# Decoder step on one core: a third staging tile for weights, and other places for weight splits and low parts around the layer norms

## The chip, the cores and the metric

The kernel runs on one core of one Trainium2 chip. The metric is device time in microseconds (us) of one execution; lower is better. The kernel before took 1143.75 us (median of three runs, 1142.8 to 1144.4).

A core has four engines that compute: TensorE (PE, matrix products), VectorE (DVE), ScalarE (ACT) and GpSimd (POOL). Each works through its own queue in order. SyncE (SP) issues the transfers between device memory and the on-chip memory. Semaphores connect the queues.

## The reference

One inference step of a decoder with two layers, in float32, on 512 prompt tokens and 8 single new tokens (520 columns), width 1024:

```
for i in range(2):
    m = attention(x) if i == 0 else gla(x)          # token mixer, with w_o
    x = layer_norm(ALPHA * x + m, ln_mix_g[i], ln_mix_b[i])
    h = x @ w_up;  a, u = halves of h               # 1024 -> 2 x 2816
    c = conv_b + causal depthwise conv, width 3, of a
    x = layer_norm(ALPHA * x + (gelu(c) * u) @ w_down, ln_ffn_g[i], ln_ffn_b[i])

layer_norm(x): mu = mean(x); var = mean((x - mu)^2)
               (x - mu) * rsqrt(var + 1e-5) * g + b
```

Layer 0 mixes tokens with sliding-window attention (16 heads, 2 key-value heads, window 128, rotary positions, sinks), layer 1 with gated linear attention (GLA, 4 heads). The caches, the GLA states and the last rows of the convolution are outputs too.

## The kernel before, in words

**Layout.** Activations lie transposed: 128 partitions hold a chunk of 128 features, 8 chunks (`KD`) make the width, and the tokens run along the free dimension. The tokens are cut in two groups, a (256 prompt tokens) and b (256 prompt tokens and the 8 samples).

**Split operands.** Matrix products run in a faster 32-bit format (`F32R`) that drops low bits. So each operand is kept as a high part (the value rounded to that format) and a low part (the value less its high part), and a product is three matmuls for each chunk: high by high, high by low, low by high (`product`, lines 193 to 196; `product2` joins the first two for group a, lines 214 and 215). For group a's first product of an FFN, `product` does all the high-by-low matmuls last (line 198).

**Units of weights.** The work is a list of units, each with one 128-column piece of a weight matrix (512 KB where it has 8 chunks). `load_unit` transfers it to a staging tile `raw` (line 160), ScalarE makes the high part `wh` (165) and VectorE the low part `wl` (168). There are `RAWS = 2` staging tiles and `WSLOTS = 6` pairs of `wh` and `wl`. A new load waits until the low part that last read its staging tile is done; a high part waits until PE has finished with its pair.

**Order.** `order` writes the sequence by hand: group a runs up to five units ahead of b within a phase, and at the end of a phase b's last units come in a row before a's first unit of the next phase. Each unit takes one slot. When b has done unit u, `next_unit` loads unit u + 6. Steps that come later are generators: each `yield n` puts the rest off by n slots (`spawn`, `due`); with `yield 0` it comes behind what is already waiting in the same slot.

This sequence is only a priority. A scheduler then lays out each engine's queue at compile time by a model of the timing: when an engine is free it takes the first step in the sequence that the model holds ready. `issue_after(ins)` ties what follows, on the engine of `ins` alone, behind `ins` in that engine's queue; it waits for nothing on other engines.

**Norms.** `ln_chunk` runs for each of the 8 chunks of the output projection (or the down projection): VectorE adds the product to x (243 or 245); after chunk 0 a first mean is taken off all chunks, held in the tiles `sb` and `sa` (251 to 258); from chunk 1 on the sum and the sum of squares over chunks grow, for group b on POOL except for the last chunk's (275, 276). Then `ln_end`: PE sums over partitions (283), ScalarE copies the mean (`mu`, 288), POOL and VectorE take it off (291, 299), VectorE and ScalarE work out the factor (292 to 305, with the exponential at 301). For each chunk VectorE then scales x (321), ScalarE adds the bias and rounds to the high part (322) and VectorE makes the low part (323).

**Weights around a norm.** A phase that begins at unit e follows a norm in three places: the FFN of layer 0, the GLA of layer 1, the FFN of layer 1. Units e + 1 to e + 5 are "late": their splits are put into the sequence one slot later, by `parts`, with the high part on ScalarE behind group a's exponential (line 177) and the low part on VectorE (179) behind a's last scaling (unit e + 1) or a's last low part (the others), as long as the slot is within `HOLD = 5` of a's norm. An FFN also holds one extra unit, e + 6, in a pair of its own; it is split without ties (165, 168).

Of the kernel before, what the change touches and what calls it, by code (L numbers as in the profile page):

```python
# [22 lines left out]
KD = 8  # L23
# [19 lines left out]
WSLOTS = 6  # L43
RAWS = 2
HIACT = 2
# [10 lines left out]
LATEB = 14  # L56

HOLD = 5

# [18 lines left out]
def parted(rows):  # L78

    return rows.rearrange("p (j t) -> p t j", t=2)  # L80
# [15 lines left out]
class Net:  # L96
# [53 lines left out]
    def load_unit(self, u, pieces=1, extra=False, late=False):  # L150
        src, nt = self.units[u][0], self.units[u][1]
        nc = self.nc
        if nt == 0:
            return self.load_rank(u)
        r = self.raw.tile([P, KD * P], F32, name="raw")
        pool = self.wx if extra else self.wts
        h, l = (pool.tile([P, KD * P], F32R, name=name) for name in ("wh", "wl"))
        n = nt * P // pieces
        for c in (slice(i * n, (i + 1) * n) for i in range(pieces)):
            nc.sync.dma_start(out=r[:, c], in_=src[:, c])  # L160
            if late:
                self.spawn(self.parts(u, h[:, c], l[:, c], r[:, c]), 1)
                continue
            if u >= HIACT:
                nc.scalar.activation(h[:, c], r[:, c], AF.Copy)  # L165
            else:
                nc.gpsimd.tensor_scalar(h[:, c], r[:, c], 1.0, 0.0, op0=ALU.mult, op1=ALU.add)
            nc.vector.tensor_tensor(l[:, c], r[:, c], h[:, c].bitcast(F32), op=ALU.subtract)  # L168
        self.w[u] = (h, l)

    def parts(self, u, h, l, r):


        norm = self.norm if self.norm and self.slot < self.norm[0] else None
        behind = lambda ins: self.tc.issue_after(ins) if norm else ExitStack()
        with behind(norm and norm[1]):
            self.nc.scalar.activation(h, r, AF.Copy)
        with behind(norm and norm[2 if u == norm[4] else 3]):
            self.nc.vector.tensor_tensor(l, r, h.bitcast(F32), op=ALU.subtract)  # L179
        yield from ()  # L180

# [47 lines left out]

    def next_phase(self):  # L230
        return min(p for p in self.phases if p > self.unit)


    def ln_chunk(self, g, m, ps, scaled, last=False):
# [7 lines left out]
        if scaled:  # L242
            nc.vector.tensor_tensor(x[:, m], x[:, m], ps, op=ALU.add)
        else:
            nc.vector.scalar_tensor_tensor(x[:, m], x[:, m], ALPHA, ps, op0=ALU.mult, op1=ALU.add)
        if m == 0:
            yield 1
            mp = self.mtile("sc")[:, :n]
            nc.tensor.matmul(mp, self.ones_a, x[:, 0], start=True, stop=True)
            sb = c("sb")  # L250
            nc.scalar.activation(sb, mp, AF.Copy, scale=float(KD))
            sa = sb
            if not scaled:
                sa = c("sa")
                nc.scalar.activation(sa, mp, AF.Copy, scale=KD / ALPHA)
# [19 lines left out]
        (nc.gpsimd if m < p1 else nc.vector).tensor_tensor(g.s1, x[:, 0] if m == 1 else g.s1, x[:, m], op=ALU.add)  # L275
        (nc.gpsimd if m < p2 else nc.vector).tensor_tensor(g.s2, g.s2, q, op=ALU.add)

    def ln_end(self, g, i, last=False):
# [25 lines left out]
        rp = r if last else e2  # L304
        nc.vector.scalar_tensor_tensor(rp, q, 1.5, r, op0=ALU.add, op1=ALU.mult)
        sc = lambda m: self.par[:, C_LNG + i * KD + m:C_LNG + i * KD + m + 1]
        bi = lambda m: self.par[:, C_LNB + i * KD + m:C_LNB + i * KD + m + 1]
        if last:
# [9 lines left out]
            return  # L318

        for m in range(KD):  # L320
            v = nc.vector.scalar_tensor_tensor(x[:, m], x[:, m], sc(m), rp, op0=ALU.mult, op1=ALU.mult)  # L321
            nc.scalar.activation(g.xh[:, m], parted(x[:, m]), AF.Identity, bias=bi(m))  # L322
            xl = nc.vector.scalar_tensor_tensor(g.xl[:, m], parted(x[:, m]), bi(m), g.xh[:, m].bitcast(F32), op0=ALU.add, op1=ALU.subtract)  # L323
        if g.i == 0:
            self.norm = self.slot + HOLD, self.exp, v.ins, xl.ins, self.next_phase() + 1
        for m in range(KD):
# [656 lines left out]

    def next_unit(self, extra):
        u = self.nu
        if u < len(self.units):
            self.nu += 1
            done = u - WSLOTS
            late = not extra and self.units[u][1] and any(e - 5 <= done < e for e in (*self.phases[2:3], *self.phases[3:4], *self.phases[5:6]))
            self.load_unit(u, extra=extra, late=late)  # L990
            if extra:
                self.extra[u] = True

    def run(self):
# [3 lines left out]
        self.attn_open()  # L998
        self.later, self.slot, self.seq, self.norm = [], 0, 0, None
        for i, u in self.order():  # L1000
            g = self.groups[i]
            _, _, f, a, pre = self.units[u]
            if i == 1:
                self.unit = u
            if i == 0 and pre:
                pre()
                if pre != self.gla_open:
                    for _ in range(EXTRA):
                        self.next_unit(True)
            self.slot += 1  # L1010
# [129 lines left out]
```

## Time and profile before

The profiled execution took 1145.38 us; its span, from the first to the last instruction, is 1143.7 us.

| | |
|---|---|
| median of three runs | 1143.75 us (1142.8 to 1144.4) |
| profiled execution | 1145.38 us, span 1143.7 us |
| PE busy | 1105.9 us, 97% of the span |
| VectorE busy | 784.1 us, 69% |
| ScalarE busy | 566.9 us, 50% |
| POOL busy | 321.8 us, 28% |
| moved by DMA | 122.81 MB, mean 107 GB/s |
| mean granted PE clock | 0.989 |

The page of the profile gives busy times, a chain of work and the costliest groups of instructions. A row of a group has line, engine, operation, output and inputs by name, shapes, count, busy time and mean. The view of waits has, for an engine: who waited for whom, the total in us, how many times, and the longest. A row of the timeline has start and duration in us, engine, line, operation, output and inputs, and in brackets the idle time of the engine just before and what ended it. A row of the windows view has a stretch, its length and, for PE, PEld (PE's weight loads), DVE, ACT and POOL, busy time and number of instructions; then the granted PE clock (1.00 is full speed), the share of the 16 DMA engines and GB/s. A matmul's end is modelled, and consecutive ones overlap, so starts are what to compare.

### The profile page before, as it was taken

The page shows a single profiled execution, that of the slowest core. Times are in us where ns is not written, and L with a number is a line of the kernel's source. Part 1 is how long each engine was busy: PE and PEld are TensorE (multiplying, and loading weights), DVE is VectorE, ACT ScalarE, POOL GpSimd, SP SyncE. Part 2 cuts the span into 40 slices and gives each one's busy share as a digit, 9 for nine tenths or more (in the row PEclk, how much of TensorE's full clock was granted, in tenths as well). Part 3 has the DMA queues.
Part 4 walks back from the last instruction along what each step waited for, and adds up shares of the span by engine and source line. Part 5 has one row for each costly group of instructions (what it writes and reads, how often), then busy time and mean ns, then how long its engine had stood idle before and what let it go on. Part 6 is the DMA issues. An engine that isn't in the chain of part 4 may idle for free.

```text
span 1143.7 us, 22908 instructions
## 1 busy us (share of the span) xinstructions
PE 1105.9 (97%) x8806; PEld 1056.7 (92%) x8806; DVE 784.1 (69%) x1628; ACT 566.9 (50%) x1251; POOL 321.8 (28%) x589
## 2 busy tenths in 40 slices
PE   8999998999999999999899999998999999999995
PEld 7997798999999999999899999898999999999994
DVE  8897578755665566568867877788755665566657
ACT  5677555534553245435545655455524553245433
POOL 4575584400110001255311100383400110011344
PEclk9999999999999999999899999999999999999998
DMA  7453022333323223242125355332333232232222
GB/s 239 150 178 93 16 75 93 111 93 119 103 93 109 94 95 109 75 132 96 56 87 162 114 176 173 118 101 92 111 98 125 93 109 95 93 112 93 75 64 75
DMA packets 53788, 122.81 MB, mean 107 GB/s; under 512 B 6792, under 2 KB 27312, under 8 KB 53680
## 3 DMA queue, kind: packets, MB, share of 16 engines
q1 hardware_dynamic: 51664, 119.61, 32.7%
q10 hardware_dynamic: 2016, 1.75, 0.5%
q8 instruction: 69, 1.13, 0.4%
q14 instruction: 39, 0.32, 0.1%
HBM read 108.67 MB, written 8.47 MB: 102 GB/s over the span
## 4 chain that ended last, share of the span: by engine, by line
PE 74%; DVE 12%; DMA 5%; ACT 3%; issue 2%; POOL 2%; SPq 0%; ACTq 0%; DVEq 0%; POOLq 0%
PE accp L214 15%; PE accp L195 15%; PE accp L193 15%; PE accp L196 15%; PE accp L215 8%; DMA vb<-dv 3%; DVE wl L168 1%; DVE xs_a L323 1%; DVE wl L179 1%; DMA raw<-in_w_up 1%; DVE sgla L877 1%; DMA raw<-in_w_qkv 1%; DVE x_a L321 1%; DMA qs<-hl 1%; PE pv L521 1%
## 5 line engine op out<-in xcount | busy, mean ns | idle before, releaser
L168 DVE TENSOR_TENSOR wl<-raw,wh 128x1024 fp32r<-128x1024 f32 (+2 forms) x174 | 210.5, 1212 | 110.5 <-ACT wh L165 109.9
L165 ACT ACTIVATE wh<-raw 128x1024 fp32r<-128x1024 f32 (+2 forms) x170 | 175.9, 1035 | 208.3 <-PE accp L195 187.2
L193 PE MATMUL accp<-xh_b,wh 128*128 128x264 f32 x976 | 271.7, 278 | 7.4 <-ACT xh_b L322 7.4
L195 PE MATMUL accp<-xl_b,wh 128*128 128x264 f32 x976 | 270.6, 278 | 0.0
L196 PE MATMUL accp<-xh_b,wl 128*128 128x264 f32 x976 | 270.5, 277 | 0.0
L214 PE MATMUL accp<-xs_a,wh 128*128 128x512 f32 x576 | 196.3, 382 | 0.0
L193 PEld LDWEIGHTS accp<-xh_b,wh 128*128 128x128 f32 x976 | 185.0, 190 | 8.3 <-ACT xh_b L322 7.8
L195 PEld LDWEIGHTS accp<-xl_b,wh 128*128 128x128 f32 x976 | 184.6, 189 | 2.5 <-issue 0.4
L196 PEld LDWEIGHTS accp<-xh_b,wl 128*128 128x128 f32 x976 | 184.4, 189 | 0.8 <-issue 0.6
L215 PE MATMUL accp<-xs_a,wl 128*128 128x256 f32 x576 | 145.4, 273 | 0.0
L193 PE MATMUL accp<-hh_b,wh 128*128 128x264 f32 x480 | 134.0, 279 | 1.7 <-ACT hh_b L221 1.2
L195 PE MATMUL accp<-hl_b,wh 128*128 128x264 f32 x480 | 134.4, 280 | 0.3 <-DVE hl_b L561 0.2
L196 PE MATMUL accp<-hh_b,wl 128*128 128x264 f32 x480 | 133.6, 278 | 0.0
L214 PEld LDWEIGHTS accp<-xs_a,wh 128*128 128x128 f32 x576 | 109.1, 189 | 11.4
L193 PE MATMUL accp<-xs_a,wh 128*128 128x256 f32 x400 | 113.6, 286 | 0.9 <-ACT wh L165 0.9
L196 PE MATMUL accp<-xs_a,wl 128*128 128x256 f32 x400 | 112.6, 284 | 1.4 <-DVE wl L168 0.8
L215 PEld LDWEIGHTS accp<-xs_a,wl 128*128 128x128 f32 x576 | 110.2, 191 | 1.9
L195 PE MATMUL accp<-xs_a,wh 128*128 128x256 f32 x384 | 109.0, 284 | 0.6 <-DVE xs_a L222 0.3
L193 PEld LDWEIGHTS accp<-hh_b,wh 128*128 128x128 f32 x480 | 91.5, 191 | 2.4 <-ACT hh_b L221 1.6
L195 PEld LDWEIGHTS accp<-hl_b,wh 128*128 128x128 f32 x480 | 91.3, 190 | 1.8 <-DVE hl_b L561 0.4
L196 PEld LDWEIGHTS accp<-hh_b,wl 128*128 128x128 f32 x480 | 91.4, 190 | 0.2
L225 POOL COPY hist<-aext 128x2 f32<-128x2 f32 x44 | 10.7, 244 | 276.8 <-DVE aext L608 274.0
(327 smaller groups left out, 2500.5 us busy)
## 6 DMA issues: line engine op xcount, KB each, us to landing
raw<-in_w_up SPq DMA_DIRECT2D x88, 512.0 KB, 3.4
raw<-in_w_down SPq DMA_DIRECT2D x32, 512.0 KB, 3.4
raw<-in_w_gla SPq DMA_DIRECT2D x24, 512.0 KB, 3.4
raw<-in_w_mix_o SPq DMA_DIRECT2D x16, 512.0 KB, 4.1
raw<-in_w_down SPq DMA_DIRECT2D x16, 384.0 KB, 3.0
qs<-hl SPq DMA_DIRECT2D x64, 64.0 KB, 2.1
sgla<-in_state_gla SPq DMA_DIRECT2D x16, 256.0 KB, 2.8
vb<-dv SPq DMA_DIRECT2D x16, 256.0 KB, 3.7
```

The source lines that it names most:

```text
L165: nc.scalar.activation(h[:, c], r[:, c], AF.Copy)
L168: nc.vector.tensor_tensor(l[:, c], r[:, c], h[:, c].bitcast(F32), op=ALU.subtract)
L179: self.nc.vector.tensor_tensor(l, r, h.bitcast(F32), op=ALU.subtract)
L193: nc.tensor.matmul(o, h[:, ks], xh, start=k == 0, stop=False)
L195: nc.tensor.matmul(o, h[:, ks], xl, start=False, stop=False)
L196: nc.tensor.matmul(o, l[:, ks], xh, start=False, stop=not tail and k == nt - 1)
L214: both = lambda: nc.tensor.matmul(o, h[:, ks], in_turn(rs[:, k].rearrange("p t q j -> p t (q j)")), start=k == 0, stop=last)
L215: low = lambda: nc.tensor.matmul(o[:, :P], l[:, ks], in_turn(rh[:, k]), start=False, stop=False)
L321: v = nc.vector.scalar_tensor_tensor(x[:, m], x[:, m], sc(m), rp, op0=ALU.mult, op1=ALU.mult)
L323: xl = nc.vector.scalar_tensor_tensor(g.xl[:, m], parted(x[:, m]), bi(m), g.xh[:, m].bitcast(F32), op0=ALU.add, op1=ALU.subtract)
L521: mm = nc.tensor.matmul(pv[64 * v:64 * v + 64, b * P:(b + 1) * P], self.vtok[:, kb, 64 * v:64 * v + 64], parts[v][w][:, b], start=i == 0, ...
L877: late(nc.vector.scalar_tensor_tensor(s[:, j], vb[:, j], kraw[:, b:b + 1], s[:, j], op0=ALU.mult, op1=ALU.add))
```

## The change

It does five things.

1. `RAWS` goes from 2 to 3: a third staging tile.
2. The tiles `sb` and `sa` of the first mean take the place of the later `nv` and `r` (same tags, one buffer each).
3. In `ln_end` the low parts of x come in a loop of their own, behind all scalings and high parts. For group a they are put off by three slots and tied, on VectorE, behind the latest add of group b, which at that point is that of b's seventh chunk.
4. Late units have a number j, 1 to 5, their distance from e, and the extra unit becomes late with j = 6. Their splits are put off by 1, 2, 2, 2, 1 and 0 slots and then come last in their slot.
5. Each j has its ties, on marks that both norms set. High parts on ScalarE: j = 1 behind a's exponential, 3 behind a's last high part, 5 and 6 behind b's exponential, 2 and 4 free. Low parts on VectorE: 1 behind a's last scaling, 2 behind a's last low part, 3 and 4 behind b's last sum of squares, 5 and 6 behind b's factor (line 305). `HOLD` and `next_phase` go.

```diff
-RAWS = 2
+RAWS = 3
...
             if late:
-                self.spawn(self.parts(u, h[:, c], l[:, c], r[:, c]), 1)
+                self.spawn(self.parts(late, h[:, c], l[:, c], r[:, c]), (0, 1, 2, 2, 2, 1, 0)[late])
                 continue
...
-    def parts(self, u, h, l, r):
-        norm = self.norm if self.norm and self.slot < self.norm[0] else None
-        behind = lambda ins: self.tc.issue_after(ins) if norm else ExitStack()
-        with behind(norm and norm[1]):
+    def parts(self, j, h, l, r):
+        for _ in range(3):
+            yield 0
+        behind = lambda what: self.tc.issue_after(self.marks[what]) if what in self.marks else ExitStack()
+        with behind({1: "exp_a", 3: "high_a", 5: "exp_b", 6: "exp_b"}.get(j)):
             self.nc.scalar.activation(h, r, AF.Copy)
-        with behind(norm and norm[2 if u == norm[4] else 3]):
+        with behind({1: "rows_a", 2: "low_a", 3: "sums_b", 4: "sums_b", 5: "factor_b", 6: "factor_b"}[j]):
             self.nc.vector.tensor_tensor(l, r, h.bitcast(F32), op=ALU.subtract)
-        yield from ()
...
-            sb = c("sb")
+            sb = c("nv")
...
-                sa = c("sa")
+                sa = c("r")
...
         for m in range(KD):
             v = nc.vector.scalar_tensor_tensor(x[:, m], x[:, m], sc(m), rp, op0=ALU.mult, op1=ALU.mult)
-            nc.scalar.activation(g.xh[:, m], parted(x[:, m]), AF.Identity, bias=bi(m))
-            xl = nc.vector.scalar_tensor_tensor(g.xl[:, m], parted(x[:, m]), bi(m), g.xh[:, m].bitcast(F32), op0=ALU.add, op1=ALU.subtract)
+            xh = nc.scalar.activation(g.xh[:, m], parted(x[:, m]), AF.Identity, bias=bi(m))
+        self.marks.update({"rows_" + g.name: v.ins, "high_" + g.name: xh.ins})
+
         if g.i == 0:
-            self.norm = self.slot + HOLD, self.exp, v.ins, xl.ins, self.next_phase() + 1
+            yield 3
+            yield 0
+        with ExitStack() if g.i else self.tc.issue_after(self.marks["add_b"]):
+            for m in range(KD):
+                xl = nc.vector.scalar_tensor_tensor(g.xl[:, m], parted(x[:, m]), bi(m), g.xh[:, m].bitcast(F32), op0=ALU.add, op1=ALU.subtract)
+        self.marks["low_" + g.name] = xl.ins
...
-    def next_unit(self, extra):
+    def next_unit(self, extra, late=0):
...
-            done = u - WSLOTS
-            late = not extra and self.units[u][1] and any(e - 5 <= done < e for e in (*self.phases[2:3], *self.phases[3:4], *self.phases[5:6]))
+            e = min((p for p in self.phases[2:4] + self.phases[5:] if p > u - WSLOTS), default=u)
+            late = late or (0 if extra else max(0, u - e))
...
                     for _ in range(EXTRA):
-                        self.next_unit(True)
+                        self.next_unit(True, WSLOTS)
```

More of the change, by code (lines that the diff above doesn't have):

```diff
@@ L56 @@
 LATEB = 14
-HOLD = 5
 WIDE = 4
@@ L228, in mtile @@
         return self.mps.tile([P, 512], F32, name=tag, bufs=2 if tag == "sc" else 1)
-    def next_phase(self):
-        return min(p for p in self.phases if p > self.unit)
     def ln_chunk(self, g, m, ps, scaled, last=False):
@@ L242, in ln_chunk @@
         if scaled:
-            nc.vector.tensor_tensor(x[:, m], x[:, m], ps, op=ALU.add)
+            add = nc.vector.tensor_tensor(x[:, m], x[:, m], ps, op=ALU.add)
         else:
-            nc.vector.scalar_tensor_tensor(x[:, m], x[:, m], ALPHA, ps, op0=ALU.mult, op1=ALU.add)
+            add = nc.vector.scalar_tensor_tensor(x[:, m], x[:, m], ALPHA, ps, op0=ALU.mult, op1=ALU.add)
+        self.marks["add_" + g.name] = add.ins
         if m == 0:
@@ L275, in ln_chunk @@
         (nc.gpsimd if m < p1 else nc.vector).tensor_tensor(g.s1, x[:, 0] if m == 1 else g.s1, x[:, m], op=ALU.add)
-        (nc.gpsimd if m < p2 else nc.vector).tensor_tensor(g.s2, g.s2, q, op=ALU.add)
+        self.marks["sums_" + g.name] = (nc.gpsimd if m < p2 else nc.vector).tensor_tensor(g.s2, g.s2, q, op=ALU.add).ins
     def ln_end(self, g, i, last=False):
@@ L304, in ln_end @@
         rp = r if last else e2
-        nc.vector.scalar_tensor_tensor(rp, q, 1.5, r, op0=ALU.add, op1=ALU.mult)
+        factor = nc.vector.scalar_tensor_tensor(rp, q, 1.5, r, op0=ALU.add, op1=ALU.mult)
+        self.marks.update({"exp_" + g.name: self.exp, "factor_" + g.name: factor.ins})
         sc = lambda m: self.par[:, C_LNG + i * KD + m:C_LNG + i * KD + m + 1]
@@ L998, in run @@
         self.attn_open()
-        self.later, self.slot, self.seq, self.norm = [], 0, 0, None
+        self.later, self.slot, self.seq, self.marks = [], 0, 0, {}
         for i, u in self.order():
@@ L1002, in run @@
             _, _, f, a, pre = self.units[u]
-            if i == 1:
-                self.unit = u
             if i == 0 and pre:
```

## The prediction

> **What bounds the kernel now.** I read the page first, then the waits of the matmul engine, then the stretches around the norms, then each engine's timeline inside them.
>
> ```profile
> span 1143.7 us, 22908 instructions
> PE 1105.9 (97%) x8806; PEld 1056.7 (92%) x8806; DVE 784.1 (69%) x1628; ACT 566.9 (50%) x1251; POOL 321.8 (28%) x589
> PE accp L193 <- ACT xh_b L322: 7.4, 2, 3.9
> PE accp L704 <- ACT v_a L771: 2.5, 1, 2.5
> PE accp L198 <- DVE xs_a L323: 0.5, 1, 0.5
> PE accp L193 <- ACT wh L165: 0.9, 2, 0.5
> PE accp L196 <- DVE wl L168: 0.8, 2, 0.5
> PE sc L473 <- ACT pr L490: 2.0, 4, 0.7
> ```
>
> TensorE (PE) is the bound: busy 97% of the span. Only its waits can be won back. The two largest groups (total, times, longest) are three waits in all, and each stands where one layer's second group of tokens (b) leaves a norm: attention to FFN, FFN to GLA, GLA to FFN. The windows view gives, for each, the idle stretch and the stretch behind it; the last row is a steady stretch for comparison (the number after POOL is the granted clock).
>
> ```profile
> 185.60:189.20 3.60, 0.14 (x2) 0.00 (x1) 3.60 (x7) 1.87 (x6) 1.98 (x4) 1.00 0.20 59
> 546.30:549.00 2.70, 0.18 (x3) 0.00 (x1) 2.65 (x10) 1.56 (x5) 0.66 (x1) 0.95 0.00 0
> 783.70:787.80 4.10, 0.16 (x3) 0.01 (x1) 4.10 (x8) 2.32 (x8) 2.48 (x5) 0.98 0.24 60
> 189.20:193.50 4.30, 4.30 (x25) 4.30 (x26) 4.30 (x12) 3.04 (x7) 0.00 (x0) 0.63 0.18 72
> 549.00:554.50 5.50, 5.50 (x18) 4.39 (x19) 5.50 (x16) 2.91 (x7) 0.00 (x0) 0.50 0.00 0
> 787.80:791.10 3.30, 3.30 (x14) 3.16 (x15) 3.30 (x10) 2.92 (x7) 0.00 (x0) 0.51 0.24 92
> 300.00:350.00 50.00, 50.00 (x380) 48.07 (x380) 32.43 (x63) 25.76 (x49) 5.55 (x22) 1.00 0.32 102
> ```
>
> Each gap is paid twice: as idle time, and again because PE comes back at a clock of 0.63, 0.50 and 0.51.
>
> Why is b's norm late? These are PE's sums over partitions for b (L283), then ScalarE's queue at all three norms:
>
> ```profile
> 175.32 0.71 PE L283 MATMUL tp<-s_b,ones_a 128*128 128x264 f32 x2 [0.42 <-DVE s_b L275]
> 536.58 0.61 PE L283 MATMUL tp<-s_b,ones_a 128*128 128x264 f32 x2
> 773.54 0.71 PE L283 MATMUL tp<-s_b,ones_a 128*128 128x264 f32 x2 [0.43 <-DVE s_b L275]
> 176.21 1.06 ACT L177 ACTIVATE wh<-raw 128x1024 fp32r<-128x1024 f32 x1 [1.96 <-DMA raw<-in_w_up]
> 178.88 1.06 ACT L177 ACTIVATE wh<-raw 128x1024 fp32r<-128x1024 f32 x1 [1.61 <-DMA raw<-in_w_up]
> 179.84 0.36 ACT L288 COPY mu<-tp 128x264 f32<-128x264 f32 x1
> 540.45 0.36 ACT L288 COPY mu<-tp 128x264 f32<-128x264 f32 x1
> 778.43 0.36 ACT L288 COPY mu<-tp 128x264 f32<-128x264 f32 x1
> ```
>
> At the first norm the mean was ready at 175.32 + 0.71 = 176.03, and its copy ran at 179.84. In between ScalarE stood in front of two weight high parts whose weights had not landed. The copy was queued behind them: 3.8 us lost. By the same subtraction it is 540.45 - 537.19 = 3.3 us at the second norm and 778.43 - 774.25 = 4.2 us at the third.
>
> **The change part by part.** *Weight parts behind marked steps.* Take the weights that follow the first of the next phase in order, 1 to 5, and the extra one, 6. High parts 5 and 6 now stand behind b's exponential on ScalarE, so they can't stand in front of the mean's copy. High part 4 has no such tie; only the third tile, below, gets it out of the way. On VectorE low parts 3 and 4 stand behind b's last sum, and 5 and 6 behind b's factor (L305). Before, VectorE ran this at the first norm:
>
> ```profile
> 165.82 1.21 DVE L179 TENSOR_TENSOR wl<-raw,wh 128x1024 fp32r<-128x1024 f32 x1
> 167.30 3.48 DVE L323 SCALAR_TENSOR_TENSOR xs_a<-x_a,par,xs_a 128x256 fp32r<-128x256 f32 x6
> 171.04 0.50 DVE L323 SCALAR_TENSOR_TENSOR xs_a<-x_a,par,xs_a 128x256 fp32r<-128x256 f32 x1
> 171.47 1.20 DVE L179 TENSOR_TENSOR wl<-raw,wh 128x1024 fp32r<-128x1024 f32 x1
> 172.94 1.43 DVE L179 TENSOR_TENSOR wl<-raw,wh 128x1024 fp32r<-128x1024 f32 x1
> 174.29 0.97 DVE L275 TENSOR_TENSOR s_b<-s_b,x_b 128x264 f32<-128x264 f32 x1
> 185.41 1.76 DVE L168 TENSOR_TENSOR wl<-raw,wh 128x1024 fp32r<-128x1024 f32 x1
> 187.43 0.43 DVE L305 SCALAR_TENSOR_TENSOR pv<-msq,r 128x264 f32<-128x264 f32 x1
> 188.10 2.08 DVE L321 SCALAR_TENSOR_TENSOR x_b<-x_b,par,pv 128x264 f32<-128x264 f32 x5
> ```
>
> Low part 3 (172.94) leaves the place in front of b's sums: 174.29 - 172.94 = 1.35 us. The extra weight's low part (185.41) leaves the place between b's statistics and its factor: 1.76 us. So b's x should be ready 3.8 + 1.35 + 1.76 = 6.9 us sooner at the first norm. PE needs it from where group a's six units end:
>
> ```profile
> 182.90 0.28 PE L193 MATMUL accp<-xs_a,wh 128*128 128x256 f32 x1
> 185.47 0.28 PE L196 MATMUL accp<-xs_a,wl 128*128 128x256 f32 x1
> 189.20 0.38 PE L193 MATMUL accp<-xh_b,wh 128*128 128x264 f32 x1 [3.46 <-ACT xh_b L322]
> ```
>
> That is 189.20 - 185.47 = 3.7 us sooner, so 3.2 us are to spare. At the second norm (no extra weight) 3.3 + 1.35 = 4.6 us stand against the 2.7 us of its window, 1.9 to spare. At the third 4.2 + 1.35 + 1.76 = 7.3 against 4.1. I take all three idle times as gone: 7.4 + 2.5 = 9.9 us. What comes next on PE is then b's own product at full rate.
>
> The clock that isn't lost: 4.30 x 0.37 = 1.6, 5.50 x 0.50 = 2.75 and 3.30 x 0.49 = 1.6 us. In the second stretch PE also waited on b's chunks one by one and on group a's GLA steps, so I take half there, 1.4. Rate term: 1.6 + 1.4 + 1.6 = 4.6 us, bounds 3.2 to 6.0.
>
> [...]
>
> *Group a's low parts behind b's seventh add.* One of the eight moves: it ran ahead of low part 1, now all come behind b's sixth and seventh adds. Beside other work six took 3.48 us, 0.58 each, so eight take 4.6. Starting some 0.8 us (two adds) after low part 1 ends at 167.0, they end near 172.4 rather than 171.54. PE reads them in the tail of a's first unit and in its second. Bounds: 0 (PE's order is laid anew) to 0.9 us a norm. Queued behind the seventh add are now these eight and low part 2; the add waits for b's seventh product, which PE finishes one unit before a's first begins, so the wait is over before VectorE gets there.
>
> *Low part 5 behind the factor.* Its weight is PE's from 182.90 on. The factor moves to 187.43 - 6.9 = 180.5 and ends by 181.0; a low part takes 1.2 us, so right behind it the part is done at 182.2 and costs nothing. Behind b's eight scalings (five take 2.08, eight 3.3) it is done at 185.5: 2.6 us of stall. Bounds 0 to 2.6 us a norm. VectorE has a gap of its own between factor and first scaling (187.86 to 188.10), which a ready part fills, so I expect the near end. For these two edits together I take 0.5 us a norm, the size of the wait that PE had on xs_a there (quoted above): 1.5 us.
>
> *Third staging tile.* A load now waits for the low part three weights back, not two. So high part 4's load waits for low part 1 (done at 167.0), not low part 2 (172.7).
>
> ```profile
> raw<-in_w_up SPq DMA_DIRECT2D x88, 512.0 KB, 3.4
> qs<-hl SPq DMA_DIRECT2D x64, 64.0 KB, 2.1
> SPq L160 <- DVE wl L168: 380.5, 81, 28.2
> 145.44 6.37 POOL L258 TENSOR_TENSOR x_b<-x_b,sa 128x264 f32<-128x264 f32 x7
> 157.97 0.42 DVE L292 SCALAR_TENSOR_TENSOR nv<-msq,pv 128x256 f32<-128x256 f32 x1 [1.22 <-ACT msq L289]
> ```
>
> With 3.4 us to landing it is there at about 170.5, ahead of the mean at 174.7 (176.03 - 1.35). That is what keeps high part 4 harmless. Elsewhere the bound is PE's pace, not the loads. PE's waits on wh and wl outside the norms are 0.9 + 0.8 = 1.7 us: gain 0 to 1.7, I take 0.5, as loads at the start can't all come sooner.
>
> *Scratch tiles sb and sa become nv and r.* Group a's nv (157.97) now has to wait until b's centring on POOL is over (151.81): 6.2 us of cover, cost 0. If POOL fell behind by more than that, a's norm would start late by the rest.
>
> *Sum.* The profiled execution took 1145.38 us (span 1143.7). 1145.4 - 9.9 - 4.6 + 1.5 - 0.5 = 1131.9. The median lies 1.63 us lower, 1143.75: forecast 1130.2 us.
>
> **The rivals.** *The stall moves to the weights' low parts.* Low part 5 misses the place right behind the factor at all three norms: 3 x 2.6 = 7.8 in place of 1.5, so 1130.2 + 6.3 = 1136.5 us. For it: VectorE is busy without a break from 185.6 to 193.5 (rows above). Against: the gap behind the factor.
>
> *The change doesn't do what it says.* The schedule puts high part 4, the untied one, ahead of the mean's copy with its load late; the wait shown at 178.88 stays, one weight earlier. Then about all the gain goes: 1143.7 us. Against: 170.5 lies 4 us ahead of 174.7.
>
> *Slower: loads in the way of the attention's transfers.* A 512 KB load issued one tile sooner lies in front of the four qs copies of a column on the same 16 DMA engines. There are 16 such steps (64 copies, four each). A load takes 3.4 us; if a third of it, 1.1 us, shows on PE each time, that costs 18 us: 1130.2 + 18 = 1148 us. It decides from 13.5 / 16 = 0.85 us a step. For: qs lands in 2.1 us, so a load ahead is felt. Against: PE waited for scores only 2.0 us in all 64 matmuls, and the queue already holds loads back 380.5 us for want of a free tile, at a pace that PE sets; a third tile shifts this once and adds no load.
>
> **How the numbers follow.** Forecast 0.70, stall at the low parts 0.15, no effect 0.08, slower 0.07. The forecast's own range: all bounds good, 1145.4 - 9.9 - 6.0 - 1.7 - 1.6 = 1126 us; all bad, with 2.6 and 0.9 us at one norm each, the smaller rate term and no gain at the start, 1145.4 - 9.9 - 3.2 + 3.5 - 1.6 = 1134. The first rival's range reaches on to 1139 (1136.5 with 0.9 us more at three norms), which makes 1126 to 1139; what is left out is the other two rivals and the tails. About 0.2% (2.3 us) can be told from no change here: faster 0.85, same 0.08, slower 0.07.
>
> **What would show it.** Right: no gap over 1 us on PE at the three places and a clock near 1.00 behind them; the mean's copy within 0.3 us of PE's sums for b; low parts 5 and 6 right behind L305. Wrong: PE waiting for wl of a's sixth unit (first rival), L177 still in front of the mean's copy, or longer waits at L473.

## The result and the profile after

The kernel after takes 1153.05 us (median of six runs, 1151.43 to 1154.91), the kernel before, beside it, 1144.08 us (1142.8 to 1147.53). The ratio is 1.0073, 95% interval 1.0058 to 1.0088: slower by 0.73%, where 1.2% faster was forecast. The profiled execution after took 1152.26 us. First its page (span and busy times), then the waits of the matmul engine (total, times, longest in us):

```profile
span 1150.6 us, 22919 instructions
PE 1110.7 (97%) x8806; PEld 1061.5 (92%) x8806; DVE 784.0 (68%) x1628; ACT 565.8 (49%) x1251; POOL 319.7 (28%) x589
```

```profile
PE accp L194 <- DVE wl L178: 3.6, 2, 1.8
PE accp L196 <- DVE xs_a L326: 2.5, 5, 0.9
PE accp L191 <- ACT hh_b L219: 2.2, 2, 1.7
PE accp L191 <- ACT wh L163: 1.9, 2, 1.4
PE accp L191 <- ACT xh_b L318: 1.3, 2, 1.0
PE accp L191 <- ACT wh L176: 1.2, 1, 1.2
```

The waits that the forecast wanted gone are gone: xh_b went from 7.4 to 1.3 us, and the 2.5 us on v_a are no longer among the large ones. In their place stand five others, grown or new, 6.7 us of them for parts of weights (wl 3.6, wh 1.9 and 1.2). The span grew by 6.9 us, and PE's busy time by 4.8 of them (1105.9 to 1110.7): most of the loss is matmuls at a lower clock (mean granted clock 0.989 before, 0.982 after), not idle time. The windows view shows where (after POOL comes the granted clock):

```profile
181.90:187.10 5.20, 1.24 (x7) 0.65 (x6) 5.17 (x11) 5.20 (x12) 0.42 (x2) 0.81 0.30 101
187.10:192.00 4.90, 4.90 (x23) 4.90 (x24) 4.90 (x13) 1.56 (x4) 0.00 (x0) 0.50 0.34 107
554.00:560.00 6.00, 5.45 (x26) 5.15 (x26) 1.52 (x3) 0.20 (x1) 0.00 (x0) 0.50 0.29 87
744.40:750.00 5.60, 5.35 (x28) 4.64 (x29) 4.60 (x9) 3.58 (x7) 0.98 (x1) 0.70 0.34 111
300.00:350.00 50.00, 50.00 (x378) 48.03 (x377) 32.96 (x63) 26.36 (x51) 6.22 (x23) 1.00 0.30 97
```

At the first norm PE now has three short gaps in 5.2 us, and then 4.9 us at half clock, more than the one gap of before (3.6 us, then 4.3 us at 0.63) had cost. The rest of the kernel (last row) runs as before.

Both traces have 8806 matmuls, so the start of the n-th of them can be compared through the whole span. The table gives by how much each stage (times of before) became longer or shorter, in us, for the kernel after and for experiments told below. It is one profiled execution each, and one execution can lie about 2 us from another in a stage: the kernel with the shared scratch alone, whose ratio can't be told from 1, shows -1.6 us to the first norm and -1.8 us at it. Verdicts go by the ratios.

| stage | after | swap | third tile alone | low 3, 4 free | low 5 free | late high parts |
|---|---|---|---|---|---|---|
| to the first norm, 0 to 170 | -0.1 | -0.3 | -0.2 | +0.2 | -0.8 | -1.7 |
| first norm, 170 to 200 | +1.0 | -2.3 | -2.6 | -4.3 | -2.2 | -4.3 |
| second norm and first GLA head, 530 to 575 | +2.2 | +0.9 | -2.3 | -2.4 | -1.2 | -3.1 |
| GLA, 575 to 738 | -1.7 | -1.2 | +2.3 | 0.0 | 0.0 | -0.1 |
| GLA's end, 738 to 746 | +4.3 | +4.6 | 0.0 | 0.0 | 0.0 | 0.0 |
| third norm, 746 to 800 | +0.9 | -1.2 | -1.6 | -2.3 | -1.7 | -3.9 |

Nothing moves between 200 and 530 or behind 800. So the loss of 6.6 us in the first column is that of norms that gained nothing and of one place that the prediction never looked at, the end of the GLA.

Why the norms gained nothing is seen on three engines. ScalarE's timeline after, at the first norm:

```profile
174.22 0.38 ACT L284 COPY mu<-tp 128x264 f32<-128x264 f32 x1
178.87 0.43 ACT L296 ACTIVATE r<-nv 128x264 f32<-128x264 f32 x1 [3.97 <-DVE nv L288]
179.77 1.28 ACT L623 ACT_TABLE_LOAD   x1
181.38 1.99 ACT L176 ACTIVATE wh<-raw 128x1024 fp32r<-128x1024 f32 x2
```

VectorE's, at the first norm, the second norm and the GLA's end:

```profile
173.46 0.43 DVE L272 TENSOR_TENSOR s_b<-s_b,sq 128x264 f32<-128x264 f32 x1
173.81 2.91 DVE L178 TENSOR_TENSOR wl<-raw,wh 128x1024 fp32r<-128x1024 f32 x2
176.64 0.97 DVE L613 SCALAR_TENSOR_TENSOR conv<-aext,par,conv 128x256 f32<-128x256 f32 x1
178.42 0.42 DVE L288 SCALAR_TENSOR_TENSOR nv<-msq,pv 128x264 f32<-128x264 f32 x1
182.31 0.44 DVE L301 SCALAR_TENSOR_TENSOR pv<-msq,r 128x264 f32<-128x264 f32 x1
182.66 1.22 DVE L178 TENSOR_TENSOR wl<-raw,wh 128x1024 fp32r<-128x1024 f32 x1
183.80 2.08 DVE L317 SCALAR_TENSOR_TENSOR x_b<-x_b,par,pv 128x264 f32<-128x264 f32 x5
185.79 1.22 DVE L178 TENSOR_TENSOR wl<-raw,wh 128x1024 fp32r<-128x1024 f32 x1
...
546.70 1.27 DVE L317 SCALAR_TENSOR_TENSOR x_b<-x_b,par,pv 128x264 f32<-128x264 f32 x3
547.90 1.69 DVE L326 SCALAR_TENSOR_TENSOR xl_b<-x_b,par,xh_b 128x264 fp32r<-128x264 f32 x4
549.52 0.68 DVE L725 TENSOR_TENSOR_SCAN dcum<-reset,dmn 128x256 f32<-128x256 f32 x1
...
742.04 0.88 DVE L880 SCALAR_TENSOR_TENSOR sgla<-vb,kraw,sgla 128x256 f32<-128x256 f32 x2 [1.98 <-DMA vb<-dv]
743.18 0.48 DVE L905 SCALAR_TENSOR_TENSOR sg<-tp,par,sg 128x256 f32<-128x256 f32 x1
```

And PE's, at the first norm and at the GLA's end:

```profile
183.43 0.38 PE L191 MATMUL accp<-xs_a,wh 128*128 128x256 f32 x1 [1.20 <-ACT wh L176]
184.90 0.39 PE L191 MATMUL accp<-xh_b,wh 128*128 128x264 f32 x1 [0.98 <-ACT xh_b L318]
187.07 0.58 PE L194 MATMUL accp<-xs_a,wl 128*128 128x256 f32 x1 [1.77 <-DVE wl L178]
...
744.31 0.49 PE L191 MATMUL accp<-hh_b,wh 128*128 128x264 f32 x2 [1.70 <-ACT hh_b L219]
```

The mean's copy stands at 174.22, 5.6 us sooner than the 179.84 of before. But nv, which needs it, comes at 178.42: VectorE first runs low parts 3 and 4 (2.9 us) and 1.8 us of the convolution's steps. So 4.2 us lie between mean and nv where before there were 1.3 (179.84 to 181.11, where nv starts in the trace of before). The second thing is in the two late parts. At 181.38 ScalarE makes two high parts in a row and VectorE two low parts, at 182.66 and 185.79. In the sequence the extra weight (6) stands ahead of weight 5: its generator was started in an earlier slot, so its parts come out one round sooner. PE needs weight 5 first, for a's sixth unit, and weight 6 only behind b's first. It waits for the second high part until 183.43 and for the second low part until 187.07. Of the 3.95 us that PE waits in this stretch 2.97 are for weight 5 and 0.98 for b's x, which comes 4.3 us sooner than before (184.90 for 189.20).

### The profile page after: what moved, and what is told of

Its sections match the earlier page's. It is cut to its first block, busy times and chain, and to the rows that moved or that the text cites. A ratio compares the mean times of both kernels' runs of the same rounds, so it can differ in the third digit from the quotient of the medians.

```text
span 1150.6 us, 22919 instructions
## 1 busy us (share of the span) xinstructions
PE 1110.7 (97%) x8806; PEld 1061.5 (92%) x8806; DVE 784.0 (68%) x1628; ACT 565.8 (49%) x1251; POOL 319.7 (28%) x589
## 4 chain that ended last, share of the span: by engine, by line
PE 74%; DVE 13%; ACT 3%; DMA 3%; issue 3%; POOL 2%; SPq 1%; ACTq 0%; DVEq 0%; POOLq 0%
PE accp L193 15%; PE accp L194 15%; PE accp L212 15%; PE accp L191 15%; PE accp L213 8%; DMA vb<-dv 2%; DVE wl L178 1%; DVE xs_a L326 1%; DVE wl L166 1%; DMA qs<-hl 1%; DVE x_b L317 1%; PE pv L524 1%; DVE sgla L880 1%; DVE x_a L317 1%; ACT pr L493 1%
## 5 line engine op out<-in xcount | busy, mean ns | idle before, releaser
L166 DVE TENSOR_TENSOR wl<-raw,wh 128x1024 fp32r<-128x1024 f32 (+2 forms) x172 | 206.3, 1201 | 104.4 <-ACT wh L163 103.5
L163 ACT ACTIVATE wh<-raw 128x1024 fp32r<-128x1024 f32 (+2 forms) x168 | 173.6, 1034 | 196.1 <-PE accp L193 194.6
L191 PE MATMUL accp<-xs_a,wh 128*128 128x256 f32 x400 | 115.8, 292 | 4.0 <-ACT wh L163 1.9
L193 PE MATMUL accp<-xs_a,wh 128*128 128x256 f32 x384 | 112.1, 293 | 0.3 <-DVE xs_a L220 0.2
```

What stands on the lines that cost most here:

```text
L191: nc.tensor.matmul(o, h[:, ks], xh, start=k == 0, stop=False)
L193: nc.tensor.matmul(o, h[:, ks], xl, start=False, stop=False)
```

## The experiments

Each is timed beside the kernel before, and the ratio is to that. None leaves out work. Letters in the texts on record name theories and rivals; theory A stands in each text for what that text says of it.

**Round one: which part of the change loses.** The swap gives the extra weight's generator one round more:

```diff
-        for _ in range(3):
+        for _ in range(3 + (j == WSLOTS)):
```

> One number is changed in the kernel after: the parts of the extra weight (6) are issued one round later in the program, so that they come behind those of weight 5, which the matmul engine needs first. Theory A (wrong order of two weights): in the kernel after, weight 6 went through ScalarE and VectorE ahead of weight 5 at the first and the third norm, and the matmul engine waited there for weight 5 (1.2 and 1.8 us at the first norm, 1.8 us at the third) and came back at half clock. Then this kernel takes 5 to 8 us less than the kernel after: 1145 to 1148 us, and the matmul engine's waits on the late wl (L178) go from 3.6 us to under 1 us. Rival B (VectorE's whole load in the window is the bound, whatever the order): 1151 to 1154 us, since the wait only passes from the weight to b's x.

Measured: 1146.22 us, ratio 1.0002 (0.9990 to 1.0015). The waits on L178 fell from 3.6 us to 1.0. That is 7 to 8 us from one number (6.8 by the medians, 0.71% by the ratios), so theory A holds. In the table 3.3 us of it stand at the first norm and 2.1 at the third; the 1.3 us at the second, which has no extra weight, are within what one execution varies. Much of it is clock: 0.982 to 0.985 in all executions of the kernel after, 0.988 to 0.995 with the swap. But it only brings the kernel back to before.

The third tile alone is the kernel before with `RAWS = 3`, `sb` as `nv` and `sa` as `r`:

> The kernel before with only the third staging tile and the two scratch tiles shared, no part tied to a step. Theory A (the third tile does little by itself, the loss of the kernel after comes from the parts that were tied to steps): 1141 to 1145 us, a little under the kernel before. Rival C (the third tile lays the order of the weights' parts anew in every stage, and that is what costs the 4 us at the end of the GLA and part of the loss at the second norm): 1147 to 1151 us, with the GLA's end about 4 us later than in the kernel before.

Measured: 1138.08 us, ratio 0.9941 (0.9924 to 0.9958). Both theories expected too little of it: the tile by itself makes the kernel 6.8 us faster. Rival C, by which it does the harm, falls. What it does at the first norm, on VectorE:

```profile
179.58 1.23 DVE L168 TENSOR_TENSOR wl<-raw,wh 128x1024 fp32r<-128x1024 f32 x1 [0.77 <-ACT wh L165]
181.12 0.42 DVE L292 SCALAR_TENSOR_TENSOR nv<-msq,pv 128x264 f32<-128x264 f32 x1
185.57 0.65 DVE L305 SCALAR_TENSOR_TENSOR pv<-msq,r 128x264 f32<-128x264 f32 x1
```

The extra weight lands sooner (its high part waits for it until 178.49; before, it ran at 184.08), its low part runs at 179.58 and no longer at 185.41, and so it doesn't stand in front of b's factor, which moves from 187.43 to 185.57. nv stays where it was (181.12): the mean's copy is still late there, so this is another gain than the one that the ties aim at. It accounts for the first norm; the 2.3 us that the table has at the second, where there is no extra weight, were not followed.

The kernel after with `RAWS = 2`, and the kernel after with group a's low parts back in the loop of the scalings:

> The kernel after with two staging tiles in place of three, all else as in the kernel after. Rival C (the third tile costs the time at the GLA's end): 1147 to 1149 us, 4 us or more under the kernel after. Theory A (the parts tied to steps are the loss; with two tiles a part held behind a step also holds the next load): the same as the kernel after or up to 6 us more, 1152 to 1159 us, with longer waits of the matmul engine on wh at the norms.

> The kernel after with group a's low parts back in the loop of the scalings, as in the kernel before; the rest of the change stays. Theory A: these low parts, held until b's seventh add, cost the matmul engine its waits on xs_a (L326; 2.5 us in five pieces) and the lower clock behind them at the third norm, so that 2 to 5 us come back there: 1148 to 1151 us; the waits on wl of weight 5 stay (3 us or more). Rival B (VectorE's load in the window is the bound, in any order): 1152 to 1154 us, the wait only moves to b's norm.

Measured: 1151.64 us, ratio 1.0059 (1.0043 to 1.0075), and 1153.90 us, 1.0078 (1.0063 to 1.0092). Neither can be told from the kernel after. So in the kernel after the third tile gives nothing that can be measured, and a's low parts, put back, give nothing either; the waits move (xs_a is no longer among PE's ten largest, wl goes from 3.6 to 4.1 us and wh of L176 from 1.2 to 2.7), as rival B said for that run.

**Round two: what the swapped kernel still loses.** With the swap: a's low parts back; no ties at the second norm; low part 4 behind b's nv.

> The kernel after with the extra weight's parts behind weight 5's (as in the run that swapped them) and group a's low parts back in the loop of the scalings. The swap alone took 6.8 us off the kernel after. Theory A (group a's held low parts cost at the first and third norm, 2.9 us of waits on xs_a and the lower clock behind them; that was hidden by the wrong order of weights 5 and 6): 1141 to 1144 us, most of the gain at the third norm. Rival B (VectorE is full between a's factor and b's scalings, so what a's low parts no longer delay, weights' low parts do): 1145 to 1148 us, as with the swap alone.

> The swapped kernel, with the parts of the weights behind the second norm (FFN to GLA) tied to no step; the first and third norm as in the swapped kernel. Theory D (at the second norm the weights' low parts 3 and 4, then 5, run ahead of group a's first decay of the GLA on VectorE; that delays the whole chain of the heads, to the GLA's last head, where the matmul engine loses 4.6 us on hh_b): the 0.9 us lost at the second norm become a gain of 1 to 2 and the loss at the GLA's end shrinks by 3 us or more: 1138 to 1142 us. Rival E (the schedule of the GLA comes out as it does for other reasons; these ties have no part in it): 1145 to 1149 us.

```diff
+        gla = self.phases[3] < self.nu <= self.phases[5]
-        behind = lambda what: ... if what in self.marks else ExitStack()
+        behind = lambda what: ... if what in self.marks and not gla else ExitStack()
```

> The swapped kernel with low part 4 behind b's nv in place of b's last sum; nothing else. Theory F (low parts 3 and 4 in front of b's nv are what keeps b's norm late): nv comes 1 to 3 us sooner at each norm than in the swapped kernel, b's x 1 us or more sooner, 1141 to 1145 us. Rival G (low part 4 is needed by the matmul engine as early as this; behind nv it comes too late and the wait passes to wl): 1146 to 1150 us with more than 1 us of new waits on L178.

```diff
-{..., 3: "sums_b", 4: "sums_b", 5: "factor_b", 6: "factor_b"}
+{..., 3: "sums_b", 4: "nv_b", 5: "factor_b", 6: "factor_b"}
```

Measured: 1148.48 us (1.0031, 1.0017 to 1.0044), 1146.57 us (1.0014, 1.0001 to 1.0028) and 1143.55 us (0.9992, 0.9980 to 1.0004), beside 1.0002 for the swap alone. The first is slower than the swap alone, against both texts: among these ties, holding a's low parts is a gain. The second changes nothing that can be told apart, so theory D, which blamed the ties of the second norm, falls. The third is in theory F's range, and nv does come 3.0 us sooner (175.22, from its trace, for 178.25), but its interval overlaps the swap's: low part 4 then stands behind nv and still in front of the factor.

The fourth kernel of this round keeps the swap and drops nearly all ties to group b: a's low parts are back in the loop, and only high parts 5 and 6 and low part 6 are tied to steps of b.

```diff
-        with behind({1: "exp_a", 3: "high_a", 5: "exp_b", 6: "exp_b"}.get(j)):
+        with behind({1: "exp_a", 2: "exp_a", 3: "exp_a", 4: "exp_a", 5: "exp_b", 6: "exp_b"}.get(j)):
-        with behind({1: "rows_a", 2: "low_a", 3: "sums_b", 4: "sums_b", 5: "factor_b", 6: "factor_b"}[j]):
+        with behind({1: "rows_a", 2: "low_a", 3: "low_a", 4: "low_a", 5: "low_a", 6: "factor_b"}[j]):
```

> Third tile, the swap, group a's low parts in the loop of the scalings; of the ties only these: high parts 5 and 6 behind b's exponential on ScalarE, low part 6 behind b's factor; high parts 1 to 4 behind a's exponential, low part 1 behind a's scalings and low parts 2 to 5 behind a's last low part, as before. Theory F (what costs is VectorE being held: low parts 3 and 4 put behind b's sums then stand in front of b's nv for 2.9 us; the ties on ScalarE are the useful part of the change): b's nv within 1 us of the mean's copy, a gain of 2 us or more at the first norm over the third tile alone, 1132 to 1137 us. Rival B (VectorE's load is the bound): 1138 to 1146 us, no better than the third tile alone (1138.1).

Measured: 1135.71 us, ratio 0.9915 (0.9896 to 0.9934): theory F's range, and the harm at the GLA's end is gone. Theory F's reason, that low parts 3 and 4 keep b's nv late, is looked at in round four.

**Round three: the parts again, with these ties.** Weight 5 moved up (high part behind the square of b's mean, low part behind b's nv); two tiles; a's low parts held as in the change; and the shared scratch alone on the kernel before.

> The kernel with only the late high parts tied (1135.7 us), with weight 5 moved up: its high part behind the square of b's mean on ScalarE in place of b's exponential, its low part behind b's nv. There the matmul engine still waited 1.1, 2.4 and 1.2 us at the three norms for low part 5, whose high part stood behind b's exponential and a table load. Theory F (order alone decides; ScalarE is free between the square and b's logarithm): the waits on L178 fall from 4.7 to under 1.5 us and the time to 1130 to 1133 us. Rival H (b's logarithm now waits behind the high part for up to 1 us, b's x comes later and the wait passes from wl to xh_b): 1135 to 1138 us.

> The kernel with only the late high parts tied (1135.7 us), with two staging tiles in place of three. Theory J (the third tile is what lets the extra weight's high and low part run before b's factor needs the engines, with or without ties): 4 to 7 us are lost, 1140 to 1143 us. Rival K (with the late high parts tied, no load stands in front of b's mean any more, and the third tile has nothing left to do): 1135 to 1138 us.

> The kernel with only the late high parts tied (1135.7 us), with group a's low parts held behind b's seventh add, as in the change. Theory L (holding a's low parts is a cost of its own: it sets a's first decay of the GLA behind b's scalings on VectorE, which the swapped kernels all showed, and leaves the matmul engine waiting for xs_a at the first and third norm): 6 to 10 us lost, 1141 to 1146 us, with the loss at the second norm and at the GLA's end. Rival M (only the held low parts 3, 4 and 5 of the weights cost): 1135 to 1138 us.

> The kernel before with only sb and sa turned into nv and r, two staging tiles. Theory N (the shared scratch costs and gains nothing; the 6.8 us of the run with third tile and shared scratch are the tile's): 1143 to 1145.5 us. Rival O (the schedule that comes out with the shared scratch is another one and has part of that gain): 1138 to 1142 us.

Measured, in this order: 1135.31 us (0.9921, 0.9905 to 0.9938), 1142.12 us (0.9976, 0.9964 to 0.9988), 1133.95 us (0.9912, 0.9895 to 0.9929), 1145.67 us (1.0006, 0.9994 to 1.0018). So: moving weight 5 up gains nothing, since the waits on L178 fall out of PE's ten largest and xh_b comes back with 2.0 us (rival H). The third tile is worth 0.61%, 7.0 us, here as well (theory J). Holding a's low parts costs nothing here (1 us under rival M's range; theory L falls). The shared scratch neither costs nor gains (theory N, 0.2 us over its range).

The kernel with a's low parts held, called "late high parts" in the table, has every part of the change except three: low parts 3, 4 and 5 are tied to group a and not to b, high parts 2 to 4 stand behind a's exponential, and weight 5 comes ahead of 6. Its VectorE, at the first and the second norm:

```profile
170.83 1.22 DVE L178 TENSOR_TENSOR wl<-raw,wh 128x1024 fp32r<-128x1024 f32 x1
171.97 0.42 DVE L240 SCALAR_TENSOR_TENSOR x_b<-x_b,accp 128x264 f32<-128x264 f32 x1
172.31 1.22 DVE L178 TENSOR_TENSOR wl<-raw,wh 128x1024 fp32r<-128x1024 f32 x1
173.44 0.42 DVE L271 TENSOR_TENSOR s_b<-s_b,x_b 128x264 f32<-128x264 f32 x1
175.86 0.43 DVE L288 SCALAR_TENSOR_TENSOR nv<-msq,pv 128x264 f32<-128x264 f32 x1
179.94 0.88 DVE L301 SCALAR_TENSOR_TENSOR pv<-msq,r 128x264 f32<-128x264 f32 x1
...
533.72 1.15 DVE L725 TENSOR_TENSOR_SCAN dcum<-reset,dmn 128x256 f32<-128x256 f32 x1
```

Low parts run around b's last add here, before the last sums. nv is 2.6 us sooner than in the kernel after, 175.86 for 178.42, and only 0.7 us behind the mean's copy (175.16 in its trace). But this execution was already 1.6 us ahead when the norm began (first row of the table), so about 1 us of it belongs to the norm. Group a's scan for the first GLA head runs at 533.72, ahead of b's scalings; in the kernel after it is at 549.52, behind them.

**Round four: which ties.** With the swap, the change's ties but low parts 3 and 4 behind a's last low part; or low part 5 alone so; the kernel "late high parts" without the swap; and that kernel with weight 5 moved up.

> The swapped kernel with low parts 3 and 4 behind a's last low part in place of b's last sum; ScalarE's ties and low part 5 behind b's factor as in the change. Theory P (low parts 3 and 4 between b's last sum and b's nv, 2.9 us of VectorE, are the tie that costs): nearly all of the 12 us between the swapped kernel and the one with only the late high parts tied come back, 1133 to 1138 us, and the second norm and the GLA's end lose nothing. Rival Q (low part 5 behind the factor, or ScalarE's ties, carry most of it): 1141 to 1147 us.

> The swapped kernel with low part 5 behind a's last low part in place of b's factor; low parts 3 and 4 behind b's last sum as in the change. Theory P: little comes back, 1144 to 1148 us, as low parts 3 and 4 still stand in front of b's nv. Rival Q (the prediction's step 'low part 5 behind the factor' is the one that fails): 1134 to 1140 us.

> The kernel with only the late high parts tied and a's low parts held (1134.0 us), without the swap, so that the extra weight's parts are issued ahead of weight 5's as in the change. Theory R (the order of weights 5 and 6 costs by itself, wherever the other low parts stand: PE waits for weight 5 at the first and the third norm): 4 to 8 us lost, 1138 to 1142 us. Rival S (the order cost only because VectorE was full with the held low parts): 1133 to 1136 us.

> The kernel with only the late high parts tied and a's low parts held (1134.0 us), with weight 5 moved up as in the run before: high part behind the square of b's mean, low part behind b's nv. Theory F: the waits on wl of 4.7 us there go, 1130 to 1133 us. Rival H (they pass to xh_b, as they did in the kernel without the held low parts, which stayed at 1135.3): 1133 to 1136 us.

Measured: low parts 3 and 4 free 1136.80 us (0.9927, 0.9908 to 0.9946); low part 5 free 1141.11 us (0.9969, 0.9958 to 0.9980); no swap 1138.80 us (0.9950, 0.9937 to 0.9962); weight 5 moved up 1134.71 us (0.9909, 0.9896 to 0.9922).

From the swapped kernel (1.0002) to "late high parts" (0.9912) it is 0.90%, 10.3 us. Freeing low parts 3 and 4 brings 0.75% of it, 8.6 us, freeing low part 5 0.33%, 3.8 us; together a little more than the whole, within the intervals. So the tie on 3 and 4 is the larger part, in theory P's range. Low part 5's 1141.11 us lie between the ranges of P and Q: it has a part of its own as long as 3 and 4 are held. Once they are free, low part 5 and the ties on ScalarE are worth 0.15% together (0.9927 to 0.9912), which can't be told from nothing.

Theory P's reason does not hold as it stands. VectorE's rows, first with the swap alone, then with low parts 3 and 4 free as well:

```profile
178.25 0.42 DVE L288 SCALAR_TENSOR_TENSOR nv<-msq,pv 128x264 f32<-128x264 f32 x1
182.15 0.44 DVE L301 SCALAR_TENSOR_TENSOR pv<-msq,r 128x264 f32<-128x264 f32 x1
540.92 2.08 DVE L317 SCALAR_TENSOR_TENSOR x_b<-x_b,par,pv 128x264 f32<-128x264 f32 x5
546.07 0.68 DVE L725 TENSOR_TENSOR_SCAN dcum<-reset,dmn 128x256 f32<-128x256 f32 x1
```

```profile
177.81 0.43 DVE L288 SCALAR_TENSOR_TENSOR nv<-msq,pv 128x264 f32<-128x264 f32 x1
181.90 0.88 DVE L301 SCALAR_TENSOR_TENSOR pv<-msq,r 128x264 f32<-128x264 f32 x1
535.68 1.15 DVE L725 TENSOR_TENSOR_SCAN dcum<-reset,dmn 128x256 f32<-128x256 f32 x1
542.90 2.08 DVE L317 SCALAR_TENSOR_TENSOR x_b<-x_b,par,pv 128x264 f32<-128x264 f32 x5
```

At the first norm b's nv and factor move by less than half a us, or by 1.0 and 0.8 us if they are counted from the start of a's low parts (165.99 and 166.52): when 3 and 4 are free they run around b's last add, the mean's copy comes at 177.11 for 174.06, and the chain is about as long. At the second norm b's scalings even come later, and a's scan 10 us sooner. PE's list of waits has no xh_b in either kernel, and 0.6 us on xl_b at the second norm in the first alone, so the 8.6 us are not won on b's norm. The table, which has somewhat more of them, puts 2.0 us at the first norm, 3.3 at the second, 3.4 in the GLA and its end and 1.1 at the third. PE's waits on q_a (1.0 us) and on hh_b at the GLA's end (1.6) are gone, those on wh of L163 fall from 1.4 to 0.5, and the mean granted clock of the profiled execution is 0.992 for 0.990; new are 2.9 us on low part 5 at the second norm. That the tie costs is shown; the way from it to these places is not.

The order of 5 and 6 costs 0.38%, 4.4 us, with the other ties gone (0.9950 for 0.9912), 7 to 8 with them (theory R). Moving weight 5 up gains nothing here either. The two best versions, 1133.95 and 1134.71 us, can't be told apart and are faster than both kernels: by 0.9% than before and 1.6% than after.

## Why the prediction was wrong, point by point

Two steps failed, of about the same size: low part 5's place behind the factor, and the place of low parts 3 and 4.

**The step that failed first: "low part 5 behind the factor … I expect the near end."** The prediction took 0.5 us a norm, for this and a's low parts together, and took it for granted that weight 5 would be the one right behind the factor. Weight 6 was, with five scalings of b between it and weight 5, and that order costs 4.4 to 8 us, shown by the swap. It could be read from the diff (the extra weight gets its place in an earlier slot, with 0 slots of delay). The first rival had this wait, at 0.15, and its sign came true (PE waiting for wl of a's sixth unit, 1.77 us at 187.07), but it priced the wait at 2.6 us a norm by b's scalings alone. The argument against it, "a gap of its own" on VectorE from 187.86 to 188.10, was a misreading: VectorE made a low part of group a there (L222, 187.77, 0.41 us). Apart from the order, the tie of low part 5 costs 3.8 us while 3 and 4 are held, 1.3 us a norm and within the bounds of 0 to 2.6.

**The second: low parts 3 and 4 "behind b's last sum".** The prediction counted the place that low part 3 left, in front of the sums, as 1.35 us won, and put the place that 3 and 4 took at nothing. On b's chain the two places cost about the same: the mean's copy came 5.6 us sooner at the first norm (3.8 + 1.35 forecast), nv only 2.7 (181.11 to 178.42), the factor 5.1 (187.43 to 182.31) and not 6.9. So of the 3.2 us to spare 1.4 were left, and low part 6, which ran in front of b's scalings, took 1.2 of these. The larger cost is off that chain: freeing the two brings 8.6 us, mostly at the second norm and the GLA's end, and how is open (round four).

**Three idle times gone, 9.9 us; clock term, 4.6 us.** The named waits did go, 7.4 + 2.5 to 1.3 + 0.5 us. As a sum over the norms it is not met by the kernel after, where new waits and half clock fill the same places. By the clock that the traces record, half clock stood for 13.7 us in all at the three norms before, and from the first to the third norm for 23.9 us after: 5.1 us more lost, where 4.6 were to be gained. In "late high parts" the sum is nearly met: the three norms are 4.3 + 3.1 + 3.9 = 11.3 us shorter, for 14.5 forecast, in an execution without any half clock there (mean granted clock 0.996; 0.993 to 0.995 in the five others of this kernel), which is in part luck.

**Third tile, 0.5 us.** Far too small: 6.8 us alone, 7.0 with the late high parts. The prediction followed the load of high part 4 and PE's waits outside the norms, and not the row that it quoted itself: the extra weight's low part at 185.41. With two tiles its load waits for the low part that ran at 177.30, and its high part came behind a table load on ScalarE, at 184.08. In the kernel after its gain can't be measured (two tiles 1.0059, three 1.0073); why was not tried.

**A's low parts behind b's seventh add, with 0 to 0.9 us a norm, and scratch, 0.** Both right in the time: 0.9912 with and 0.9915 without the hold, and 1.0006 for the scratch. PE's waits on xs_a did grow in the kernel after, from 0.5 to 2.5 us, 2.0 of them at the third norm and so above the bound there, but putting the low parts back gave nothing.

**The other rivals.** "No effect" falls: high part 4 ran at 169.06 at the first norm, five us ahead of the mean's copy. "Slower" ended on the right side by luck: the attention did not slow down (-0.1 us to the first norm), so loads in front of qs cost nothing that shows.

**The GLA's end, not in the prediction at all.** 4.3 us there. VectorE's step on the states (L880, at 742.04) waited 1.98 us for the transfer of vb; the gate (L905) is queued behind it and hh_b needs the gate, so PE stood 1.70 us and went on at 0.70 of its clock. The loss goes with how far a's first scan of the GLA (L725) falls behind b's factor on VectorE. In the kernel after it starts 7.1 us behind it (549.52, the factor at 542.44 in its trace); 5.3 to 8.4 us in the six others that show the loss (swap, two tiles, a's low parts back with and without the swap, no ties at the second norm, low part 4 behind nv). It starts ahead of the factor, or at most 4.4 us behind, in all that don't show it. How a delay at 550 becomes one at 740, with a GLA in between that is 1.2 to 2.5 us faster in the seven, is not settled; that it is removed by freeing 3 and 4, or 5, is shown.

## What to carry to other kernels

A step that is tied behind another one isn't gone: write down, for each one, between which two steps it now stands, and charge its time there before counting what its old place gives back. Then look at what else waits in the same engine's queue, for the other group too: here the tie cost little on the chain that it was meant to help and much elsewhere. And when several parts are moved together, list the order in which they come out against the order in which the consumer needs them; one wrong pair cost here as much as the best part of the change gained.

## What the hardware showed that was not expected

The clock that PE got back after a gap did not follow from the gap's length here. In "late high parts" and in the same kernel without the swap PE waits 2.42 us for the same weight at the second norm. The windows of gap and of what follows, first for the one, then for the other:

```profile
537.85:540.27 2.42, 0.01 (x2) 0.01 (x1) 2.42 (x6) 0.76 (x3) 0.40 (x1) 1.00 0.00 0
540.27:544.00 3.73, 3.73 (x32) 3.63 (x32) 3.73 (x11) 2.35 (x6) 0.00 (x0) 1.00 0.49 139
```

```profile
541.60:544.02 2.42, 0.00 (x0) 0.00 (x1) 2.42 (x6) 0.77 (x3) 0.40 (x1) 1.00 0.00 0
544.02:548.00 3.98, 3.98 (x21) 3.98 (x22) 3.98 (x11) 2.60 (x6) 0.00 (x0) 0.57 0.42 135
```

The same idle time is followed by full clock in the one and by 0.57 for 4 us in the other, which costs 3.98 x 0.43 = 1.7 us. What decides between the two, no run shows. The half clock also comes in one length in the traces of before and after: from the first norm to the third each stretch of it lasts 3.41 us or twice that (before: 190.32 to 193.73, 548.72 to 555.54, 787.65 to 791.06; after: 185.13 to 191.96, 553.77 to 560.60, 744.92 to 748.33, 775.64 to 779.05, 792.71 to 796.12), at 0.50 in each and 1.00 just ahead of it and behind it. The 0.57 over 3.98 us in the second kernel here is as much: 3.98 x 0.43 / 0.5 = 3.4 us at half clock. Each 3.41 us at half clock lose 1.7 us. So a forecast for this kernel should carry the clock behind a gap of this length as 0 or 1.7 us, or 3.4 as behind the 2.5 us wait of the kernel before at its second norm, and take a stage of one execution as uncertain by that much.
